# The first layer's squares: POOL adds them in whole tiles, queued behind DVE's splits of the input

## The chip, the cores and the metric

The kernel runs on one core of a Trainium2 chip. The metric is the device time of one execution in microseconds (us); the median of three executions of the kernel before is 2201.84 us (2200.74 to 2202.67). In what follows PE is the engine for matrix products (TensorE), DVE is VectorE, ACT is ScalarE, POOL is GpSimd and SP is SyncE, which here only issues transfers. Each engine takes its instructions strictly in the order in which they stand in its queue, and an instruction that waits holds up all that stands behind it on that engine.

## The reference, cut to what matters

The program is a decoder trunk of two layers over 1024 tokens and 1024 features, float32. Only the start of the first layer matters here:

```python
def rmsnorm(x, g):
    xf = x.astype(jnp.float32)
    var = jnp.mean(xf * xf, axis=-1, keepdims=True)
    return (xf * lax.rsqrt(var + EPS)).astype(x.dtype) * g
...
    for l in range(DEPTH):
        h = rmsnorm(x, norm_mix_g[l])
        uv, z, xbc, dt_raw, c_q, c_kv, k_rope = split_cols(h @ w_in[l])
...
        x = x + mix @ w_out[l]
        x = x + squared_relu_mlp(rmsnorm(x, norm_mlp_g[l]), mlp_w1[l], mlp_w2[l])
    return rmsnorm(x, final_norm_g)
```

The row factor rsqrt(var + EPS) is a scalar for each token, so the kernel multiplies x·g by the weights first and scales the product by it afterwards. The sum of squares is thus needed only when the first product is taken out of PSUM.

## The kernel before

The input lies transposed: eight tiles `x` of 128 features by 1024 tokens (m = 0 to 7), each loaded in two halves of 512 tokens. A float32 product is made of three fast products of split numbers: every operand a becomes a_hi (a rounded copy, written by ACT) and a_lo = a - a_hi (written by DVE). For the input this is `norm_in`: ACT writes `hThi` (line 256), and DVE writes `hTlo` (line 257; the profile gives the helper's line, L103). For the weights it is `split`: ACT's `whi` (L115), DVE's `wlo` (L100).

The first product of the layer is `zps`, eight tiles of 128 tokens by 422 columns, 24 matmuls each (8 feature tiles by 3). The first four token tiles (`z_start`) need the first halves of the input alone, the other four (`z_rest`) the second halves too.

Beside the splits, ACT squares each half of each x tile (`sq_half`), and the squares of the eight feature tiles are summed into one tile: 13 additions of 128x512 on POOL and the last one on DVE (L100, `sq<-sq`). PE then sums over the partitions with a product by ones (`pss`, two columns for each of the eight token tiles), DVE makes the reciprocal root from it in thirteen small steps (`rv`, `ry`, `rt`, `rh`), and only then can ACT take the `zps` tiles out of PSUM (`z_evac`: `zt`, `dk`). Behind the first four of these on ACT stand the splits of the weights of the next product, `xbc`. `row_bcast` (`rb`) spreads the row factor by PE.

The order on each engine is set by a scheduler at build time, which simulates the program; within one engine it may move instructions past each other where data allow it. `tc.issue_after(ins)` tells it that what stands in the block goes, on the engine of `ins` alone, behind `ins`.

Of the kernel before, what the change touches and what calls it, by code (L numbers as in the profile page):

```python
# [9 lines left out]
F32 = mybir.dt.float32  # L10
# [8 lines left out]
P = 128  # L19
# [3 lines left out]
KD = D // P  # L23
# [44 lines left out]
def trunk(ctx, tc, x, w_zdk, w_uv, w_f, w_q, w_kv, w_out, w1, w2, gains, pcol, prow, w_s, cst, out):  # L68
# [5 lines left out]
    small = ctx.enter_context(tc.tile_pool(name="small", bufs=4))  # L74
# [4 lines left out]
    def G(dt=F32, name="g"):  # L79
        return gp.tile([P, 1024], dt, tag="g", name=name)  # L80
# [14 lines left out]
    dve = nc.vector  # L95
    pool = nc.gpsimd
    pe = nc.tensor

    def tt(o, a, b, op, eng=None):
        (eng or dve).tensor_tensor(out=o, in0=a, in1=b, op=op)  # L100
# [10 lines left out]
    def f(ap):  # L111
        return ap.bitcast(F32)
# [121 lines left out]
    def weights(n, ahead=0):  # L234
        a = taken[0]
        prefetch(a + n + ahead)
        taken[0] = a + n
        r = loaded[a:a + n]
        for i in range(a, a + n):
            loaded[i] = None  # L240
        return r
# [11 lines left out]
    def norm_in(xm, m, gi, hT, a=0, b=S):  # L253
        hi, lo = (hsl(h, m, a, b) for h in hT)
        g = gcol[:, gi, m:m + 1]
        act.activation(hi, xm[:, a:b], AF.Copy, scale=g)
        stt(lo, xm[:, a:b], g, f(hi), ALU.mult, ALU.subtract)

    def sq_add(acc, xm, m, a=0, b=S):
        sq = G(F32, "sq")  # L260
        act.activation(sq[:, a:b], xm[:, a:b], AF.Square, scale=1.0 / 32.0)
        if m == 0:
            acc.append(sq)
        else:
            tt(acc[0][:, a:b], acc[0][:, a:b], sq[:, a:b], ALU.add, pool if m < KD - 1 else dve)
# [10 lines left out]
    def hsl(h, k, a, b):  # L276
        return h[:, k * S + a:k * S + b]
# [34 lines left out]
    def begin(l):  # L312
        L = Layer()
        L.l = l
        L.hT = (BIG(F32R, "hThi"), BIG(F32R, "hTlo"))
        L.sq = []
        L.zt = list(range(NT)) if l == 0 else [4, 5, 6, 7, 0, 1, 2, 3]
        L.dk = small.tile([P, NT, 38], F32, tag="dk", name="dk", bufs=1)
        L.rh = small.tile([P, NT], F32, tag="rh1", name="rh1", bufs=1)
        return L  # L320

    def z_start(L, k):
        if k == 0:
            L.zo = [PA("zps") for _ in range(4)]
        for t in range(4):
            z_mm(L, L.zo[t], t, k)
# [587 lines left out]
    def half(n):  # L914
        return slice(n * 512, n * 512 + 512)
# [150 lines left out]
    def sq_half(acc, xm, m, n, eng=None):  # L1066
        if m == 0 and acc:
            act.activation(acc[0][:, half(n)], xm[:, half(n)], AF.Square, scale=1.0 / 32.0)
            return
        sq = G(F32, "sq")  # L1070
        act.activation(sq[:, half(n)], xm[:, half(n)], AF.Square, scale=1.0 / 32.0)  # L1071
        if m == 0:
            acc.append(sq)
        else:
            tt(acc[0][:, half(n)], acc[0][:, half(n)], sq[:, half(n)], ALU.add, eng)
# [151 lines left out]
    L = begin(0)  # L1227
    xs = []

    def x_load(n):  # L1230
        while len(xs) < min(n, 2 * KD):
            h, m = divmod(len(xs), KD)
            xs.append(xs[m] if h else G(F32, "x"))
            nc.sync.dma_start(out=xs[m][:, half(h)], in_=x[m * P:(m + 1) * P, half(h)])
# [4 lines left out]
    for m in range(KD):  # L1239
        x_load(m + 4)  # L1240
        if m % 2 == 0:
            (L.wz[m // 2],) = weights(1, 0)
        norm_in(xs[m], m, 0, L.hT, 0, 512)
        sq_half(L.sq, xs[m], m, 0, pool)
        if m >= 1:
            z_start(L, m - 1)
    consts()
    z_start(L, KD - 1)
    for m in range(KD):
        x_load(KD + m + 4)  # L1250
        norm_in(xs[m], m, 0, L.hT, 512, S)
        sq_half(L.sq, xs[m], m, 1, pool if m < KD - 1 else dve)
    xs.clear()
    for l in range(DEPTH):
        last = l == DEPTH - 1
        xsrc = x if l == 0 else xd
# [45 lines left out]
        L = attention(L, l, xsrc).go()  # L1302
# [75 lines left out]
```

## Time and profile before

| | |
|---|---|
| median of three executions | 2201.84 us |
| the profiled execution | 2201.31 us, of which its span is 2199.5 us |
| PE busy | 2171.2 us, 99% of the span |
| DVE, ACT, POOL busy | 1661.8, 1138.0 and 477.2 us |
| mean granted clock of TensorE | 0.997 |

The span runs from the first to the last instruction. Every time of a row is counted from the span's start. A row of several merged instructions gives the start of the first and the time in which one of them ran. "idle before" in square brackets is the time in which the engine stood still ahead of the row, with what ended it.

### The profile page before, as it was taken

To read this page: it belongs to the slowest core of one execution; us is meant where nothing else is said; L and a number is where in the kernel's file an instruction comes from. 1 tells how busy PE (TensorE), PEld (TensorE's weight loads), DVE (VectorE), ACT (ScalarE), POOL (GpSimd) and SP (SyncE) were. 2 spreads that over 40 slices of the span, in tenths; PEclk is the share of its full clock that TensorE was granted. 3 is DMA by queue.
4 is the path that set the end of the run, shared out by engine and by line. 5 is a ranking of instruction groups with operands and counts; after the bars stand their busy time and mean duration, and the time that the engine had idled before them with its cause. 6 is when DMAs were issued, how large, how long until landed. Compare 5 with 4: busy or idle time off the path is not lost.

```text
span 2199.5 us, 28731 instructions
## 1 busy us (share of the span) xinstructions
PE 2171.2 (99%) x10844; PEld 1846.9 (84%) x10844; DVE 1661.8 (76%) x2484; ACT 1138.0 (52%) x1867; POOL 477.2 (22%) x451
## 2 busy tenths in 40 slices
PE   9999999999999999999999999999999999999997
PEld 8888989888888888888898889998888888888886
DVE  7788588888776876767847867878888767677576
ACT  6364477556445445355533625775464453553543
POOL 4152266221010001001301613761110010011002
PEclk9999999999999999999999999999999999999999
DMA  5211301445565546545412113023565565356532
GB/s 175 75 53 57 87 1 48 98 125 138 121 130 138 128 100 140 147 89 125 156 50 70 54 45 75 1 96 68 135 153 122 106 140 147 88 125 144 136 75 77
DMA packets 64922, 222.16 MB, mean 101 GB/s; under 512 B 7600, under 2 KB 7952, under 8 KB 64784
## 3 DMA queue, kind: packets, MB, share of 16 engines
q0 software_dynamic: 20736, 75.51, 20.2%
q1 hardware_dynamic: 44048, 144.83, 19.9%
q8 instruction: 85, 1.39, 0.3%
q14 instruction: 53, 0.43, 0.1%
HBM read 211.87 MB, written 8.44 MB: 100 GB/s over the span
## 4 chain that ended last, share of the span: by engine, by line
PE 93%; DVE 4%; issue 2%; ACT 1%; DMA 1%; POOL 0%; SPq 0%; POOLq 0%; ACTq 0%; DVEq 0%
PE st L1014 60%; PE cqkv L119 5%; PE xbc L119 5%; PE uvps L119 4%; PE av L119 4%; PE sc L119 3%; PE zps L119 2%; PE pTp L805 2%; PE qps L119 2%; PE yps L119 1%; PE vps L119 1%; PE knps L119 1%; DVE hB L103 1%; DMA x<-in_x 1%; DVE mx L767 1%
## 5 line engine op out<-in xcount | busy, mean ns | idle before, releaser
L1014 PE MATMUL st<-bhi,wlo 128*128 128x512 f32 x2016 | 785.1, 389 | 0.0
L1014 PE MATMUL st<-blo,whi 128*128 128x512 f32 x2016 | 785.0, 389 | 0.0
L1014 PE MATMUL st<-bhi,whi 128*128 128x512 f32 x2016 | 778.1, 390 | 2.4 <-ACT bhi L115 2.4
L1014 PEld LDWEIGHTS st<-bhi,whi 128*128 128x128 f32 x2016 | 378.7, 188 | 81.1 <-ACT bhi L115 2.7
L1014 PEld LDWEIGHTS st<-blo,whi 128*128 128x128 f32 x2016 | 378.9, 188 | 78.7 <-DVE blo L100 0.5
L1014 PEld LDWEIGHTS st<-bhi,wlo 128*128 128x128 f32 x2016 | 378.7, 188 | 78.5
L206 POOL DMA_DIRECT2D ssum<-in_w x96 | 84.1, 876 | 937.5 <-DVE wlo L100 387.5
L100 DVE TENSOR_TENSOR wlo<-raw,whi 128x1024 fp32r<-128x1024 f32 (+4 forms) x189 | 237.2, 1256 | 54.2 <-issue 29.8
L100 DVE TENSOR_TENSOR x<-x,st 128x512 f32<-128x512 f32 x296 | 196.7, 683 | 30.2 <-PE st L1014 29.8
L115 ACT CAST bhi<-tsum 128x1024 fp32r<-128x1024 f32 x96 | 101.0, 1052 | 213.9 <-DVE tsum L100 172.9
L115 ACT CAST whi<-raw 128x1024 fp32r<-128x1024 f32 (+4 forms) x189 | 193.9, 1029 | 16.0 <-DVE blo L100 12.3
L107 POOL TENSOR_SCALAR p<-p,sm 128x1024 f32<-128x1024 f32 (+6 forms) x84 | 158.9, 1901 | 113.0 <-DVE sm L790 81.3
L115 ACT CAST whi<-ssum 128x1024 fp32r<-128x1024 f32 x108 | 113.4, 1050 | 116.3 <-DMA ssum<-in_w 50.2
L100 DVE TENSOR_TENSOR wlo<-ssum,whi 128x1024 fp32r<-128x1024 f32 x108 | 132.1, 1223 | 49.9 <-ACT whi L115 28.9
L100 DVE TENSOR_TENSOR blo<-tsum,bhi 128x1024 fp32r<-128x1024 f32 x96 | 117.4, 1223 | 46.7 <-ACT bhi L115 46.3
L119 PE MATMUL av<-pT,vhi 128*128 128x256 f32 x480 | 113.5, 298 | 0.7 <-DVE pT L100 0.4
L1059 ACT ACTIVATE hid<-hid 128x1024 f32<-128x1024 f32 x64 | 67.8, 1060 | 87.0 <-DVE hid L1052 86.8
L1052 DVE CUSTOM_DVE_ANT_0 hid<-st,hid 128x512 f32<-128x512 f32 x96 | 65.3, 689 | 56.3 <-PE st L1014 55.9
L119 PE MATMUL sc<-B 96*128 96x384 f32 (+11 forms) x432 | 100.9, 351 | 3.2 <-ACT p L780 1.9
L100 POOL TENSOR_TENSOR sq<-sq 128x512 f32<-128x512 f32 x44 | 67.0, 1528 | 159.7 <-ACT sq L1071 157.6
L780 ACT ACTIVATE p<-sc,mx 128x512 f32<-128x512 f32 (+3 forms) x144 | 83.3, 583 | 20.7 <-DVE mx L100 14.2
L100 DVE TENSOR_TENSOR blo<-hB,bhi 128x1024 fp32r<-128x1024 f32 x48 | 58.7, 1223 | 46.5 <-ACT bhi L115 46.5
(248 smaller groups left out, 3649.7 us busy)
## 6 DMA issues: line engine op xcount, KB each, us to landing
raw<-in_w SPq DMA_DIRECT2D x128, 512.0 KB, 3.9
ssum<-in_w POOLq DMA_DIRECT2D x96, 512.0 KB, 5.7
ssum<-in_w SPq DMA_DIRECT2D x32, 512.0 KB, 4.5
raw<-in_w POOLq DMA_DIRECT2D x32, 512.0 KB, 7.9
raw<-in_w_f SPq DMA_DIRECT2D x20, 512.0 KB, 3.8
raw<-in_w_out SPq DMA_DIRECT2D x16, 512.0 KB, 3.6
dec<-adr SPq DMA_DIRECT2D x16, 384.0 KB, 3.4
ssum<-in_w_out POOLq DMA_DIRECT2D x12, 512.0 KB, 5.8
```

The costliest lines, as they stand in the source:

```text
L100: (eng or dve).tensor_tensor(out=o, in0=a, in1=b, op=op)
L103: dve.scalar_tensor_tensor(out=o, in0=a, scalar=s, in1=b, op0=op0, op1=op1)
L107: (eng or dve).tensor_scalar(out=o, in0=a, scalar1=s1, scalar2=None, op0=op0)
L115: act.copy(hi, src)
L119: pe.matmul(o, lhsT=l, rhs=r, start=start, stop=stop)
L206: pool.dma_start(out=o, in_=src, accum_op=ALU.add)
L767: dve.reduce_max(mx[:, n:n + 1], on, axis=AX.X, negate=True)
L780: act.activation(pw[:, n * wh:(n + 1) * wh], os[n][:, :wh], AF.Exp, bias=mx[:, 0:1], accum_out=sm[:, n:n + 1])
L805: pe.transpose(pt[:, c0:c0 + P], pp[j][:, kt * P:(kt + 1) * P], ident)
L1014: pe.matmul(os[j], lhsT=w[:, cw], rhs=b[:, cb], start=first and n == 0, stop=last and n == 2, skip_group_check=True)
L1052: dve._custom_dve(TENSOR_ADD_SAT, out=d, in0=os[j], in1=d, s0=0.0 if full[0] else BIGGEST, s1=-BIGGEST if full[0] else 0.0)
L1059: act.activation(d, d, AF.Square)
```

## The change

The squares no longer follow each half of the input. After all splits have been queued, one POOL instruction copies a single column out of the second half of `hTlo` of feature tile 5 (`mark`), so it has to wait for that split. All POOL additions of squares are queued behind it, and squares and additions are now whole tiles of 128x1024 (`sq_add`, which the kernel already had): eight squares on ACT, six additions on POOL, one on DVE.

```diff
     for m in range(KD):
...
         norm_in(xs[m], m, 0, L.hT, 0, 512)
-        sq_half(L.sq, xs[m], m, 0, pool)
         if m >= 1:
             z_start(L, m - 1)
...
         norm_in(xs[m], m, 0, L.hT, 512, S)
-        sq_half(L.sq, xs[m], m, 1, pool if m < KD - 1 else dve)
-    xs.clear()
+    mark = small.tile([P, 1], F32, tag="mark", name="mark", bufs=1)
+    behind = pool.tensor_copy(mark, f(hsl(L.hT[1], 5, 512, 513)))
+    with tc.issue_after(behind.ins):
+        for m in range(KD):
+            sq_add(L.sq, xs[m], m)
+            xs[m] = None
```

On POOL, at the start of the program, the queue differs as follows (- before, + after; `wst` and `Cz` are later work). The row `L100 ISA` is an instruction that the build puts ahead of POOL's first tensor_tensor: it reloads POOL's library of routines.

```order
+L1377 UNCONDITIONAL_BRANCH
+L1252 COPY mark<-hTlo 128x1
 L100 ISA
-L100 TENSOR_TENSOR sq<-sq 128x512 x13
+L100 TENSOR_TENSOR sq<-sq 128x1024 x6
 L100 TENSOR_TENSOR wst<-wst,cs 128x512
 L416 MEMSET Cz 64x1024 x2
```

Before, the reload was POOL's first work behind the branch and the additions came straight after it; now both stand behind `mark`.

On ACT, from the weights' casts to the second half of feature tile 5, the queue of the changed kernel reads so (`x_105`, `x_110`, `x_112`, `x_114`, `x_132`, `x_152`, `x_174` and `x_190` are the feature tiles 0 to 7; the rows show the stretch from tile 5's first half on, without the two casts of constants that follow `sq_306`).

```order
L256 ACTIVATE hThi_101<-x_152,gcol_75 128x512
L256 ACTIVATE hThi_101<-x_105,gcol_75 128x512
L261 ACTIVATE sq_301<-x_105 128x1024
L256 ACTIVATE hThi_101<-x_110,gcol_75 128x512
L261 ACTIVATE sq_303<-x_110 128x1024
L256 ACTIVATE hThi_101<-x_112,gcol_75 128x512
L261 ACTIVATE sq_306<-x_112 128x1024
```

Behind these stand the two casts of constants, `hThi` of tiles 6 and 7 (first halves), `hThi` and the square of tile 3, `hThi` and the square of tile 4, and then `hThi` of tile 5's second half. Only POOL's instructions are queued behind `mark`; ACT's squares stand among the splits as before, five whole ones ahead of that `hThi`.

On PE, around the matmuls that read the sum of squares, before (the last four of eight `pss`; the name in brackets is the engine whose semaphore is waited for):

```order
L119 MATMUL zps<-whi,hThi 128x422
L119 MATMUL pss<-ones,sq 128x2 [waits DVE_49]
L119 MATMUL pss<-ones,sq 128x2 x3
L119 MATMUL zps<-wlo,hThi 128x422
L119 MATMUL zps<-whi,hTlo 128x422
```

and in the changed kernel (all eight `pss`):

```order
L119 MATMUL zps<-whi,hTlo 128x422
L119 MATMUL pss<-ones,sq 128x2 [waits DVE_49,PE_49]
L119 MATMUL pss<-ones,sq 128x2 x7
L119 MATMUL zps<-whi,hThi 128x422 [waits DVE_49]
L119 MATMUL zps<-wlo,hThi 128x422
```

Before, four `pss` stood further up and four here, with 38 `zps` behind them; now all eight stand in one place, with 24 `zps` (the last token tile) behind them, whose first waits for DVE's reading of `pss`. Later in the program only some neighbours in the attention stages of both layers change places.

## Rows read from the trace of the kernel before

**Rows 1.** The page's head and its row on PE.

```profile
span 2199.5 us, 28731 instructions
PE 2171.2 (99%) x10844; PEld 1846.9 (84%) x10844; DVE 1661.8 (76%) x2484; ACT 1138.0 (52%) x1867; POOL 477.2 (22%) x451
```

**Rows 2.** What PE waited for in the first 60 us: total, times, longest.

```profile
PE zps L119 <- DVE hTlo L103: 0.7, 1, 0.7
PE zps L119 <- DVE wlo L100: 0.5, 1, 0.5
```

**Rows 3.** POOL in order of time: start, us, then the instructions.

```profile
9.21 1.34 POOL L100 TENSOR_TENSOR sq<-sq 128x512 f32<-128x512 f32 x1 [8.77 <-ACT sq L1071]
11.86 7.46 POOL L100 TENSOR_TENSOR sq<-sq 128x512 f32<-128x512 f32 x4 [1.30 <-ACT sq L1071]
20.95 13.83 POOL L100 TENSOR_TENSOR sq<-sq 128x512 f32<-128x512 f32 x8 [1.64 <-ACT sq L1071]
```

**Rows 4.** DVE's splits of the input in order of time.

```profile
4.90 0.75 DVE L103 SCALAR_TENSOR_TENSOR hTlo<-x,gcol,hThi 128x512 fp32r<-128x512 f32 x1 [3.89 <-ACT hThi L256]
...
20.14 11.61 DVE L103 SCALAR_TENSOR_TENSOR hTlo<-x,gcol,hThi 128x512 fp32r<-128x512 f32 x8
```

**Rows 5.** By tile: duration in ns of one, min/median/max (sq; then x).

```profile
L100 POOL TENSOR_TENSOR sq<-sq x44: 1276/1618/2000, 9.2 to 2173.8; 128x512 f32<-128x512 f32 x44
...
L103 DVE SCALAR_TENSOR_TENSOR hTlo<-x,gcol,hThi x16: 737/1770/1786, 4.9 to 33.6; 128x512 fp32r<-128x512 f32 x16
```

**Rows 6.** PE in order of time: the last pss, and xbc's first use of wlo.

```profile
39.33 0.95 PE L119 MATMUL pss<-ones,sq 128*128 128x2 f32 x8
...
50.19 0.62 PE L119 MATMUL xbc<-hThi,wlo 128*128 128x512 f32 x2
```

**Rows 7.** The chain that ended last, its piece behind the last pss.

```profile
40.27 7.37 PE zps L119 x38
```

**Rows 8.** ACT in order of time, first 50 us.

```profile
4.14 0.72 ACT L256 ACTIVATE hThi<-x,gcol 128x512 fp32r<-128x512 f32 x1 [1.82 <-DMA x<-in_x]
...
14.87 0.73 ACT L256 ACTIVATE hThi<-x,gcol 128x512 fp32r<-128x512 f32 x1 [0.61 <-DMA x<-in_x]
...
19.18 0.28 ACT L169 CAST ident_r<-cs 128x128 fp32r<-128x128 f32 x1
...
19.57 0.72 ACT L256 ACTIVATE hThi<-x,gcol 128x512 fp32r<-128x512 f32 x1
20.20 0.61 ACT L1071 ACTIVATE sq<-x 128x512 f32<-128x512 f32 x1
20.71 0.71 ACT L256 ACTIVATE hThi<-x,gcol 128x512 fp32r<-128x512 f32 x1
...
42.99 0.58 ACT L372 ACTIVATE zt<-zps,rh 128x384 f32<-128x384 f32 x1 [14.33 <-DVE rh L107]
...
47.42 2.07 ACT L115 CAST whi<-raw 128x1024 fp32r<-128x1024 f32 x2
49.30 0.68 ACT L372 ACTIVATE zt<-zps,rh 128x384 f32<-128x384 f32 x1
```

**Rows 9.** DVE's split of xbc's first weights.

```profile
48.58 1.23 DVE L100 TENSOR_TENSOR wlo<-raw,whi 128x1024 fp32r<-128x1024 f32 x1 [0.42 <-ACT whi L115]
```

**Rows 10.** By tile, 128x1024: a POOL addition (csq), a DVE subtraction (blo).

```profile
L100 POOL TENSOR_TENSOR csq<-csq x6: 2356/2410/2424, 197.5 to 1324.4; 128x1024 f32<-128x1024 f32 x6
...
L100 DVE TENSOR_TENSOR blo<-tsum,bhi x96: 1215/1225/1228, 505.6 to 2168.1; 128x1024 fp32r<-128x1024 f32 x96
```

**Rows 11.** Behind a wait of PE in layer 1: timeline, window (busy, clock), weight loads.

```profile
1580.72 1.16 PE L119 MATMUL rb<-cs,ry 128*128 128x128 f32 x8 [1.71 <-DVE ry L103]
...
1582.20:1585.60 3.40, 3.40 (x10) 0.50 0.37 148
...
L1014 PEld LDWEIGHTS st<-bhi,wlo x15: 187/188/331, 1574.9 to 1589.7; 128*128 128x128 f32 x15
```

## The prediction

> **What bounds the kernel now.** I read the page first. PE is busy for 2171.2 of 2199.5 us [rows 1], so the time is PE's work plus its few idle stretches, and nothing that happens on POOL, DVE or ACT counts unless PE has to wait for it. All of the change lies in the first 50 us, so I then read what PE waits for there. That is little: 0.7 us for a split of the input (`hTlo`) and 0.5 us for a split of weights [rows 2]. This is the most that the change can win, about 1.2 us, or 0.05%.
>
> The timelines of POOL and DVE show what makes these splits late. Alone, a split takes 0.75 us [rows 4], and its shortest is 737 ns; the median of the sixteen is 1770 ns [rows 5]. Eight in a row take 11.61 us from 20.14 on [rows 4], 1.45 each, while eight POOL additions run beside them for 13.83 us, 1.73 each [rows 3], against a shortest of 1.276 [rows 5]. The two slow each other. So DVE would be served if POOL kept still. But the sum of squares has its own reader: PE's last `pss` begin at 39.33 [rows 6], and behind them the chain goes on through DVE's root and ACT's `zt`, which starts at 42.99 after 14.33 us of standing still [rows 8]. The question is when the additions end now, and what PE has left to do until then.
>
> **The change part by part.**
>
> *Squares on ACT.* Eight whole squares replace sixteen halves. Two halves at a pace of 0.51 (20.20 to 20.71) are 1.02 us; a whole tile, priced by the two casts of 128x1024 that take 47.42 to 49.30, is 0.94 [rows 8]. That wins ACT some 0.6 us in all, on an engine that PE doesn't wait for: nothing on the path.
>
> *When `mark` is free.* It waits for DVE's split of tile 5's second half. ACT's `hThi` of that half sets it, as DVE, without POOL beside it, keeps up. ACT last waits for a transfer at 14.87; between there and this `hThi` stand eight `hThi` at 0.63 (19.57 to 20.20), five whole squares at 0.94 and two casts of constants at 0.39 together (19.18 to 19.57) [rows 8]: 5.04 + 4.70 + 0.39 = 10.1, so it starts at 25.0. A split of the input ends 1.51 after its `hThi` starts (4.14 to 4.90 + 0.75) [rows 4, 8]: 26.5. The copy of one column is of no weight.
>
> *The reload of POOL's library.* This is the part that neither the title nor the diff shows. Before, it lay in the 8.77 us in which POOL idles ahead of its first addition [rows 3], and that addition waited for ACT's square, so the reload cost nothing. Now it stands behind `mark`, and the additions behind it. Its price L has no row: it lies between 0 and 8.8 us, the gap that hid it. No duration in the trace is of the same kind, so I take the middle, 4.4, and keep both ends.
> The Trainium skill has a price (GPSIMD Engine Reference, section Instruction dispatch): the first call after a library is loaded pays about 6 us that no instruction in the profile shows. The trace neither bears this out nor excludes it, since the gap of 8.77 us would have hidden it [rows 3]; by that figure the sum below ends near 2212.5.
>
> *Six additions.* A POOL addition of 128x1024 takes 2.36 to 2.42 us [rows 10]: six make 14.4. They start at 26.5 + L and end at 40.9 + L. If L is under about 3 us, the last two splits run beside them; each such split stretches a half-tile addition from 1.28 to 1.74 [rows 3, 5], so 0.9 more; with L = 4.4 they are past, and DVE has nothing else to do. DVE's own last addition of 128x1024 is 1.22 [rows 10]. The sum of squares is ready at 42.1 + L.
>
> *PE until then.* Before, it came to the last four `pss` at 39.33 [rows 6], with 38 `zps` behind them [rows 7]. Now 24 stand behind them, so 14 more come before: 14 x 0.194 (7.37 / 38) = 2.7 us. Against this, four `pss` are no longer among them (0.95 us for four [rows 6]) and the waits of 1.2 us [rows 2] are gone. PE arrives at about 39.9 and stands still for 2.2 + L us, 6.6 with L = 4.4.
>
> *Behind the wait.* Eight `pss` in place of four: 1.9 us. From the end of `pss` (40.27 [rows 7]) the old chain took until 49.81 to have the first `wlo` of `xbc` (48.58 + 1.23 [rows 9]): DVE's root, four `zt` on ACT, the cast, the split, 9.54 us. Before, PE had 38 `zps` to fill this; now it has 24, 4.7 us, and `rb`, and it waits again, for the weights. PE used that `wlo` at 50.19 [rows 6]; it will do so at 42.1 + L + 1.9 + 9.5 = 53.5 + L. The loss is 3.3 + L.
>
> *The clock.* Elsewhere a wait of PE of 1.71 us was followed by a granted clock of 0.50, the lower of the two levels (1.2 GHz), for 3.4 us, and a weight load took up to 331 ns in place of 187 [rows 11]. After a wait of 6.6 us I expect the same. The eight `pss`, which are mostly weight loads, then take 1.9 x 331 / 187 = 3.3 us, 1.4 more. The `zps` behind them get slower too, but PE is early for `xbc`, which hides that. Bounds: 0, and 2.6 if all the 3.4 us go at a pace of 331 to 187 and ACT's chain doesn't hide it, with a second fall at the wait for the weights.
>
> *The rest of the program.* PE's other waits follow from its own products, so a delay here is carried to the end; the few matmuls that change places in attention I cost at nothing, give or take 1 us: what hides them is that PE has a queue of other matmuls there, and without it they would cost a fraction of a us each.
>
> **The sum.** 3.3 + 4.4 + 1.4 = 9.1 us. The profiled execution took 2201.31, 0.5 under the median; 2201.84 + 9.1 = 2211.0 us, 0.4% slower.
>
> **The rivals.**
>
> *The reload is cheap* (L under 3). For it: nothing in the rows shows such a load, and no transfer is needed if the routines are there already. Then the loss is 3.3 + 0.9 + 1.4 = 5.6 with L = 0, 2207.4; without the fall of the clock 4.2, 2206.0. It is still a loss, since POOL alone needs 14.4 us.
>
> *PE doesn't wait at all* (the other side). The splits come earlier, PE's 1.2 us of waits go, and the additions end in time: 2201.84 - 1.2 = 2200.6, no change that can be measured. It decides at an end of the additions at 39.9 - 1.2 = 38.7, so at (38.7 - 26.5) / 6 = 2.0 us each with no reload at all. Against it stand six rows with 2.36 as the shortest [rows 10].
>
> *It is worse than summed*: the reload fills the whole gap of 8.8, or the clock falls twice, or late `zt` keep PSUM tiles that PE wants. 3.3 + 8.8 + 1.4 = 13.5, 2215.3; with 2.6 for the clock 2216.5.
>
> **How the numbers follow.** The forecast (L from 3 to 8) has 0.57, the cheap reload 0.26, no wait 0.06, the worse one 0.11. Two runs of this kernel can be told apart by about 0.2%, 4.4 us: faster means under 2197.4, slower over 2206.2. No case goes under 2197.4; I leave 0.02 for what the attention stages may do. The cheap reload without a fall of the clock lies just under 2206.2 and takes a fifth of its 0.26; with the case without a wait that makes 0.11 for the same, and 0.87 for slower. The range from 2205.5 to 2215.5 holds the forecast, the cheap reload and a part of the worse one.
>
> **What the changed profile would show.** Right: POOL's six additions of about 2.4 us each, the first one some us after `mark`; the splits on DVE at 0.75 us, the last before 31; one wait of PE of over 4 us at `pss` for DVE's `sq`, a second, shorter one at `xbc` for ACT's `whi` or DVE's `wlo`, and from there on the same intervals as before. L is the gap on POOL between `mark` and the first addition. Wrong: additions that end before 39, a PE that doesn't stand still at `pss`, or a delay at 50 us that is gone again at the end.

## The result, and the profile after

The changed kernel takes 2215.37 us (median of 4 executions, 2212.5 to 2215.74), the kernel before 2201.36 in the same comparison: a ratio of 1.0062, 95% interval 1.005 to 1.0075. The change costs 14.0 us. Behind the forecast of 2211.0 stood a loss of 9.1; the time is inside the range and near its upper end. The profiled execution took 2215.74 us.

The page of the changed kernel, head and row on PE (for [rows 1]):

```profile
span 2214.0 us, 28706 instructions
PE 2180.9 (99%) x10844; PEld 1851.3 (84%) x10844; DVE 1654.6 (75%) x2484; ACT 1138.6 (51%) x1859; POOL 470.5 (21%) x445
```

The span is 14.5 us longer, but PE's busy time grew by 9.7 us with the same 10844 matmuls. A wait alone would leave the busy time as it was, so some of the matmuls must have become slower.

POOL in order of time, 20 to 50 us (for [rows 3]):

```profile
27.11 0.19 POOL L1252 COPY mark<-hTlo 128x1 f32<-128x1 f32 x1 [26.67 <-DVE hTlo L103]
27.34 15.55 POOL L100 TENSOR_TENSOR sq<-sq 128x1024 f32<-128x1024 f32 x6
```

The six additions begin 0.04 us after the copied column ends (27.11 + 0.19 = 27.30), although the reload of POOL's library stands between the two.

DVE in order of time, 26 to 48 us (for [rows 4]):

```profile
26.29 0.75 DVE L103 SCALAR_TENSOR_TENSOR hTlo<-x,gcol,hThi 128x512 fp32r<-128x512 f32 x1 [0.81 <-ACT hThi L256]
27.86 2.43 DVE L103 SCALAR_TENSOR_TENSOR hTlo<-x,gcol,hThi 128x512 fp32r<-128x512 f32 x1 [0.81 <-ACT hThi L256]
30.21 2.46 DVE L107 TENSOR_SCALAR cw<-pc 128x25 f32<-128x25 f32 x2
32.59 0.74 DVE L103 SCALAR_TENSOR_TENSOR hTlo<-x,gcol,hThi 128x512 fp32r<-128x512 f32 x1
...
42.93 1.23 DVE L100 TENSOR_TENSOR sq<-sq 128x1024 f32<-128x1024 f32 x1 [9.61 <-POOL sq L100]
47.88 0.17 DVE L107 TENSOR_SCALAR rv<-pss 128x8 f32<-128x8 f32 x1 [3.73 <-PE pss L119]
```

The splits take 0.75 us each until POOL starts to add; the next one then takes 2.43, and the last one, which starts 0.03 us ahead of POOL's third addition, 0.74 again. That addition by itself:

```profile
32.62 2.95 POOL L100 TENSOR_TENSOR sq<-sq 128x1024 f32<-128x1024 f32 x1
```

DVE then idles 9.61 us until POOL's sixth addition has ended.

What PE waited for in the first 100 us (for [rows 2]):

```profile
PE pss L119 <- DVE sq L100: 5.1, 1, 5.1
PE zps L119 <- ACT whi L115: 0.5, 1, 0.5
PE zps L119 <- DVE rv L107: 0.3, 1, 0.3
```

PE in order of time (for [rows 6]):

```profile
44.30 3.55 PE L119 MATMUL pss<-ones,sq 128*128 128x2 f32 x16 [5.10 <-DVE sq L100]
...
57.44 0.73 PE L119 MATMUL xbc<-hThi,wlo 128*128 128x512 f32 x2
...
64.07 0.63 PE L119 MATMUL xbc<-hTlo,whi 128*128 128x512 f32 x2
...
65.47 0.63 PE L119 MATMUL xbc<-hTlo,whi 128*128 128x512 f32 x2
```

The wait for a split of the input is gone, and a wait of 5.1 us stands at `pss` in its place. The first use of xbc's `wlo` came 7.25 us later than before (50.19 in [rows 6]). That is half of the loss. The other half is not in the first 60 us. The last two rows show where to look: six matmuls start in 1.40 us, 233 ns each. The same product in the trace of before, PE in order of time:

```profile
59.80 0.62 PE L119 MATMUL xbc<-hThi,wlo 128*128 128x512 f32 x2
...
61.63 0.62 PE L119 MATMUL xbc<-hThi,whi 128*128 128x512 f32 x2
```

Eight matmuls in 1.83 us, 229 ns each. The same shows in the table by tile, PE's `xbc` (count, then duration in ns of one, min/median/max), of before and then of the changed kernel:

```profile
L119 PE MATMUL xbc<-hTlo,whi x160: 388/392/397, 49.7 to 1190.2; 128*128 128x512 f32 x160
```

```profile
L119 PE MATMUL xbc<-hTlo,whi x160: 388/395/397, 56.7 to 1202.4; 128*128 128x512 f32 x160
```

And the clock of the changed kernel by windows (length, busy time of PE, PEld, DVE, ACT, POOL, then the granted clock, DMA share, GB/s; for [rows 11]):

```profile
39.30:41.40 2.10, 0.00 (x0) 0.00 (x0) 0.00 (x0) 0.00 (x0) 2.02 (x2) 1.00 0.00 0
41.45:51.60 10.15, 7.04 (x26) 6.81 (x27) 3.41 (x14) 1.03 (x3) 1.44 (x1) 0.50 0.01 2
51.70:55.00 3.30, 3.30 (x21) 3.24 (x21) 2.04 (x9) 3.30 (x11) 0.00 (x0) 1.00 0.00 0
505.55:508.90 3.35, 3.35 (x10) 2.67 (x10) 2.48 (x4) 1.53 (x2) 0.00 (x0) 0.51 0.54 203
1492.15:1495.50 3.35, 3.35 (x10) 2.69 (x9) 3.17 (x5) 2.95 (x6) 1.45 (x1) 0.50 0.44 148
```

The clock fell to its lower level (0.50, 1.2 GHz) while PE stood still at `pss`, and stayed there for 10 us. Two short falls follow later in this execution, where before had one [rows 11]. A short fall costs about 1.6 us (`st` matmuls of 0.43 us from start to start in place of 0.23, eight of them).

What sets the matmuls' pace can't be a wait, since PE is busy throughout. What differs is where the operands lie. In the built kernels the tile pool of the weights (`gp`) lies in SBUF behind the pool of small tiles, and `mark`, 4 bytes per partition, takes 32 there. `hThi` and `hTlo` are 32768 bytes per partition each, a tile of `gp` 4096, all whole multiples of 128, so what is left of a distance when multiples of 128 are taken off (the last column) is the same for every pair of a split input and a weight tile:

```text
byte address per partition    hThi    gp starts   distance mod 128
before                        22336   97536       64
changed                       22336   97568       96
```

So the theory that the experiments were to test has two parts: the order makes PE wait (about half), and the copied column shifts the weights by 32 bytes, which slows the products of the split input (the rest). The rivals: the loss is all due to the wait and what it sets off, or the order is innocent and the whole tiles are what costs.

### The profile page after: what moved, and what is told of

Same layout as the page of the kernel before. It is cut to its first block, busy times and chain, and to the rows that moved or that the text cites. A ratio compares the mean times of both kernels' runs of the same rounds, so it can differ in the third digit from the quotient of the medians.

```text
span 2214.0 us, 28706 instructions
## 1 busy us (share of the span) xinstructions
PE 2180.9 (99%) x10844; PEld 1851.3 (84%) x10844; DVE 1654.6 (75%) x2484; ACT 1138.6 (51%) x1859; POOL 470.5 (21%) x445
## 4 chain that ended last, share of the span: by engine, by line
PE 92%; DVE 3%; issue 2%; ACT 1%; POOL 1%; POOLq 0%; ACTq 0%; DVEq 0%
PE st L1014 60%; PE cqkv L119 5%; PE xbc L119 5%; PE uvps L119 4%; PE av L119 4%; PE sc L119 3%; PE pTp L805 2%; PE qps L119 2%; PE zps L119 2%; PE yps L119 1%; PE vps L119 1%; PE knps L119 1%; POOL sq L100 1%; DVE hB L103 1%; DVE mx L767 1%
## 5 line engine op out<-in xcount | busy, mean ns | idle before, releaser
L100 DVE TENSOR_TENSOR wlo<-raw,whi 128x1024 fp32r<-128x1024 f32 (+4 forms) x189 | 235.2, 1246 | 54.2 <-issue 29.8
L100 DVE TENSOR_TENSOR x<-x,st 128x512 f32<-128x512 f32 x296 | 196.3, 681 | 30.5 <-PE st L1014 30.1
L100 DVE TENSOR_TENSOR wlo<-ssum,whi 128x1024 fp32r<-128x1024 f32 x108 | 131.9, 1221 | 49.7 <-ACT whi L115 27.5
L100 DVE TENSOR_TENSOR blo<-tsum,bhi 128x1024 fp32r<-128x1024 f32 x96 | 117.4, 1223 | 46.6 <-ACT bhi L115 46.3
L780 ACT ACTIVATE p<-sc,mx 128x512 f32<-128x512 f32 (+3 forms) x144 | 83.3, 583 | 21.0 <-DVE mx L100 14.5
L100 DVE TENSOR_TENSOR blo<-hB,bhi 128x1024 fp32r<-128x1024 f32 x48 | 58.7, 1222 | 46.5 <-ACT bhi L115 46.5
L100 POOL TENSOR_TENSOR sq<-sq 128x512 f32<-128x512 f32 (+1 forms) x37 | 60.3, 1634 | 147.6 <-ACT sq L1071 145.8
```

The lines of the kernel that those rows point to most:

```text
L780: act.activation(pw[:, n * wh:(n + 1) * wh], os[n][:, :wh], AF.Exp, bias=mx[:, 0:1], accum_out=sm[:, n:n + 1])
```

## The experiments

**Shifts alone.** First, the changed kernel with 64 bytes in place of 4 for the copied column:

```diff
-    mark = small.tile([P, 1], F32, tag="mark", name="mark", bufs=1)
-    behind = pool.tensor_copy(mark, f(hsl(L.hT[1], 5, 512, 513)))
+    mark = small.tile([P, 16], F32, tag="mark", name="mark", bufs=1)
+    behind = pool.tensor_copy(mark[:, 0:1], f(hsl(L.hT[1], 5, 512, 513)))
```

> The changed kernel, with the copied column in a tile of 64 bytes a partition in place of 4, so that the tiles laid out behind it in SBUF stand 64 bytes further on than in the kernel before, and not 32. Theory A (the shift by 32 bytes is what makes the matmuls of xbc and cqkv start every 233 ns in place of 229): they start every 229 ns again, the creep of about 4 us over these four stages is gone, and the time is near 2211. The start of the program stays: PE waits about 5.1 us at pss, and the first use of xbc's wlo is at about 57.4. Theory B (another cause, such as other buffers or other neighbours in the queues): 233 ns stay, and the time is near 2215. A fall of the clock more or less behind the waits of the later stages moves either by 1.6 us.

Measured: 2206.95 us (1.0025 of before, 1.0015 to 1.0035), 8.4 under the changed kernel. PE in order of time, and its `xbc` by tile:

```profile
43.78 3.55 PE L119 MATMUL pss<-ones,sq 128*128 128x2 f32 x16 [5.05 <-DVE sq L100]
...
57.72 0.62 PE L119 MATMUL xbc<-hThi,wlo 128*128 128x512 f32 x2
```

```profile
L119 PE MATMUL xbc<-hTlo,whi x160: 389/389/398, 57.2 to 1197.3; 128*128 128x512 f32 x160
```

The wait and the late `wlo` are unchanged, and 8.4 us went all the same, by faster matmuls: 389 ns, under the 392 of before. That is twice the 4 us that the expectation had, since it counted on the 229 ns of before and not on a pace that before never had. Then the kernel before, with nothing but a tile of 4 bytes added:

```diff
+    pad = small.tile([P, 1], F32, tag="mark", name="mark", bufs=1)
+    pool.memset(pad, 0.0)
```

> The kernel before, with one more 4-byte tile that POOL sets to zero at the start, so that everything laid out behind it stands 32 bytes further on; no queue is changed otherwise. Theory A (the shift slows xbc and cqkv): matmuls of these two every 233 ns in place of 229, 960 of them, so 4 us more, near 2205.5, and nothing changed before 49 us. Theory B (it was something else): 229 ns, and 2201.4. A fall of the clock more or less moves either by 1.6 us.

Measured: 2206.69 us (1.0022, 1.0013 to 1.0032). PE's `xbc` by tile:

```profile
L119 PE MATMUL xbc<-hTlo,whi x160: 392/396/397, 49.9 to 1194.8; 128*128 128x512 f32 x160
```

An unused tile costs 5.6 us, with no new wait in the first layer. With 64 bytes, `[P, 16]`, in place of 4:

> The kernel before, with 64 unused bytes per partition ahead of the tiles of the weights and no other change; the squares are as before. Theory A (the place of the weights in SBUF sets the pace of the matmuls): as under the changed kernel with 64 bytes, the matmuls of xbc and cqkv go at about 227 ns from start to start in place of 229, some 1.7 us in each layer, 2197.5 us, 0.998. Theory B (the changed kernel's gain with 64 bytes had to do with its own 32 bytes alone, and nothing is below the pace of before): 229 ns and no change, 2201.1.

Measured: 2198.64 us (0.9988, 0.9979 to 0.9997), 2.5 us faster. PE's `xbc` by tile:

```profile
L119 PE MATMUL xbc<-hTlo,whi x160: 389/389/398, 48.3 to 1188.2; 128*128 128x512 f32 x160
```

These four kernels make a table in which the two parts add:

| us | weights shifted by 32 bytes | by 64 bytes | what 32 costs over 64 |
|---|---|---|---|
| squares as before | 2206.69 | 2198.64 | 8.1 |
| squares as changed | 2215.37 | 2206.95 | 8.4 |
| what the new order of squares costs | 8.7 | 8.3 | |

Against the unshifted kernel before, 5.6 us of the 14.0 belong to the shift and 8.3 to 8.7 to the squares. The rival that it is all the wait is refuted.

Two more shifts, one execution each, ask what the pace depends on. 96 bytes ahead of the weights (`[P, 24]`):

> The kernel before with 96 unused bytes ahead of the tiles of the weights. Theory A (32 bytes modulo 64 is what is slow): the matmuls of xbc and cqkv go at 233 ns from start to start and the time is near 2206, as with 32 bytes. Theory B (the nearer to a whole multiple of 128 the input and the weights lie to each other, the faster): with 96 bytes they are 32 apart, as near as with 32 bytes but on the other side, which also gives 233. Either is refuted by a pace of 227 to 229. The run tells whether the pattern is of period 64.

64 bytes ahead of nearly everything, so that weights and split input move together:

```diff
+    pad = const.tile([P, 16], F32, name="pad")
+    pool.memset(pad[:, 0:1], 0.0)
```

> The kernel before with 64 unused bytes ahead of all tiles but the first constants, so that weights and split input move together. If the distance between the two counts: pace as before, 229 ns for xbc and cqkv and 233 for uvps, 2201. If the place of the weights alone counts: as with 64 bytes ahead of the weights alone, 227 and 228.6 ns, 2198.5. A third outcome (slower than 229) would say that the input's place counts too.

Measured: 2205.92 and 2200.8 us. PE's `xbc` by tile, with 96 bytes and then with all moved:

```profile
L119 PE MATMUL xbc<-hTlo,whi x160: 392/395/399, 47.7 to 1192.6; 128*128 128x512 f32 x160
```

```profile
L119 PE MATMUL xbc<-hTlo,whi x160: 388/392/398, 47.9 to 1190.0; 128*128 128x512 f32 x160
```

96 bytes are as slow as 32, and when both operands move by 64, nothing changes, while 64 for the weights alone gave 389. So in these runs the distance between the two operands counts, not the place of either: modulo 128, a distance of 0 gives 389 ns, 64 gives 392, and 32 or 96 give 395 to 396. That is `xbc`'s pattern. `uvps`, another product of the split input, has it only in part: it was slow before already and gains at a distance of 0 alone. Before, and then with 64 bytes ahead of the weights:

```profile
L119 PE MATMUL uvps<-whi,hTlo x128: 388/394/398, 105.6 to 1253.1; 128*128 128x512 f32 x128
```

```profile
L119 PE MATMUL uvps<-whi,hTlo x128: 387/389/402, 103.7 to 1250.2; 128*128 128x512 f32 x128
```

The products `st`, whose operands lie in `gp` both and so at a distance of 0, keep a mean of 389 to 391 ns whether the weights are shifted or not. That fits; distances that differ by 128 bytes alone were not run, so the period of 128 is a reading of these four distances.

**All additions on DVE**, in whole tiles and in the queue's old place, without a copied column (weights not shifted):

```diff
-            tt(acc[0][:, a:b], acc[0][:, a:b], sq[:, a:b], ALU.add, pool if m < KD - 1 else dve)
+            tt(acc[0][:, a:b], acc[0][:, a:b], sq[:, a:b], ALU.add, dve)
```

> The squares as whole tiles as in the changed kernel, but all seven additions on DVE, no copy to wait for and no POOL addition in the first layer; the layout is that of the kernel before. Theory A (what costs is that POOL needs about 15 us from the fifth second-half split on): DVE adds a tile in 1.15 to 1.22 us between its splits, the sum is ready by about 34, PE comes to pss at about 39 to 40 and does not wait, the first use of xbc's wlo comes 0.5 to 1.5 us earlier than the 50.2 of before, and the time is 2200 to 2201.4. Rival (the splits are held up by DVE's additions, so that PE waits for hTlo instead): waits of PE for hTlo of over 1 us before 35, and a time of 2202 to 2204.

Measured: 2201.02 us (0.9998, 0.9989 to 1.0008). DVE's last addition, and what PE waited for in the first 100 us:

```profile
30.90 1.22 DVE L100 TENSOR_TENSOR sq<-sq 128x1024 f32<-128x1024 f32 x1
```

```profile
PE warm L119 <- DVE eps L162: 1.1, 1, 1.1
PE xbc L119 <- ACT whi L115: 0.3, 1, 0.3
```

On DVE an addition of a whole tile takes 1.22 us against 2.4 on POOL [rows 10], and the sum is ready 12 us earlier than in the changed kernel. Both waits of before are gone, and xbc's first `wlo` came at 48.92, 1.3 us earlier than 50.19. The total did not move. The clock doesn't explain that: each of the two traces has one short fall, this one near 392 and before near 1582. But the 1.3 us are no sure gain either: in the four kernels that keep the squares as before and only shift tiles, the same matmul came at 50.39, 48.76, 48.15 and 48.33, so single traces differ there by 2 us.

**The wait filled.** The kernel with 64 bytes, with 24 unused matmuls ahead of `pss` for PE to do while it waits, and token tile 6 as the last one of `zps`:

```diff
     def sq_rstd(acc, tag, t0=0, t1=NT, tg="c", fill=None):
         n = t1 - t0
         pss = bank(tg, "pss")
+        if fill:
+            for _ in range(24):
+                mm(pss[:, 64:486], hsl(fill[1], 7, 512, 640), hsl(fill[0], 7, 512, 934), True, True)
```

> The changed kernel with the 64-byte tile, and 24 matmuls whose results are not used put into PE's wait ahead of pss (the token tiles of the first layer are queued in the order 4, 5, 7, 6, which is the order that the scheduler made anyway). Theory A (the clock fell because PE stood still, and the eight pss at the lower clock cost 3.55 us in place of 1.75): no fall of the clock near 41, pss in about 1.75 us, the first use of xbc's wlo at about 55.6 in place of 57.4, and the time 1.5 to 2 us under that of the same kernel without the filling. Rival (the clock's fall is hidden behind ACT's chain, or pss take 3.5 us for another reason): 57.4 and no difference.

Measured: 2206.39 us (1.0022, 1.0013 to 1.0032). PE in order of time, then a window (columns as above):

```profile
39.34 4.78 PE L119 MATMUL pss<-hThi,hTlo 128*128 128x422 f32 x24
44.05 1.95 PE L119 MATMUL pss<-ones,sq 128*128 128x2 f32 x16
...
55.57 0.73 PE L119 MATMUL xbc<-hThi,wlo 128*128 128x512 f32 x2
```

```profile
46.45:49.80 3.35, 3.35 (x10) 3.17 (x11) 1.83 (x11) 1.08 (x3) 0.00 (x0) 0.50 0.00 0
```

With PE busy until 44.05, the eight `pss` took 1.95 us in place of 3.55, so the lower clock had cost 1.6 there; xbc's `wlo` came 2.15 us earlier (57.72 to 55.57). A shorter fall came none the less, a little later. The median moved only 0.56 us, inside the interval, so of the clock only these 1.6 us on `pss` are shown, and not what it costs the whole.

**The order, or the whole tiles?** Whole tiles on POOL without the order, without the copied column (weights not shifted):

```diff
     for m in range(KD):
         x_load(KD + m + 4)
         norm_in(xs[m], m, 0, L.hT, 512, S)
-    mark = small.tile([P, 1], F32, tag="mark", name="mark", bufs=1)
-    behind = pool.tensor_copy(mark, f(hsl(L.hT[1], 5, 512, 513)))
-    with tc.issue_after(behind.ins):
-        for m in range(KD):
-            sq_add(L.sq, xs[m], m)
-            xs[m] = None
+    for m in range(KD):
+        sq_add(L.sq, xs[m], m)
+        xs[m] = None
```

> Whole squares, six additions on POOL and one on DVE, as in the changed kernel, but not ordered behind the splits, and without the copied column, so that the tiles lie as before. If the order is what makes PE wait: POOL adds while the squares come, the sum is ready before 39, PE doesn't stand still at pss for more than a few tenths, 2201 us, within 0.1 per cent. If the whole tiles do it (POOL's first addition can only begin with the second half of tile 1, and its additions stretch beside DVE's splits to 3 us or more): the sum is ready near 43, PE waits 3 us at pss, 2204.5 to 2206.

Measured: 2210.82 us (1.0037, 1.0025 to 1.005), five executions from 2205.87 to 2211.05; the profile is of the first, at a mean granted clock of 0.997, the longest had 0.993. POOL, DVE, and PE's waits in the first 60 us:

```profile
18.24 16.43 POOL L100 TENSOR_TENSOR sq<-sq 128x1024 f32<-128x1024 f32 x6 [17.80 <-ACT sq L261]
```

```profile
18.81 17.07 DVE L103 SCALAR_TENSOR_TENSOR hTlo<-x,gcol,hThi 128x512 fp32r<-128x512 f32 x7 [0.81 <-ACT hThi L256]
```

```profile
PE zps L119 <- DVE hTlo L103: 3.4, 2, 1.9
PE xbc L119 <- ACT whi L115: 1.4, 1, 1.4
```

Both theories fall short here. The sum is ready in time and PE doesn't wait at `pss`, but the splits beside the whole-tile additions take 2.4 to 2.9 us each, against 0.75 alone (the row has six of them and one behind POOL's last addition, 2.44 on average), and PE waits for the splits, 3.4 us, and for weights. So the order does what it was made for: whole tiles on POOL without it cost about as much, by another wait. The trace is of the fastest execution, 4.7 us over before; what the slower ones have on top of it is not shown. Next, the order with halves in place of whole tiles (64 bytes):

```diff
     with tc.issue_after(behind.ins):
-        for m in range(KD):
-            sq_add(L.sq, xs[m], m)
-            xs[m] = None
+        for n in range(2):
+            for m in range(KD):
+                sq_half(L.sq, xs[m], m, n, pool if m < KD - 1 or n == 0 else dve)
```

> Halves of the squares as before, ordered behind the split of tile 5 as in the changed kernel, with 64 bytes for the copied column. If the order is what makes PE wait: 13 additions of 1.28 us behind the copied column take 16.6 us in place of 14.4, the sum is ready about 1 us later than with whole tiles and 64 bytes, whose wait was 5.05 us, so the wait is 5 to 6.5 us and the time 2207 to 2208.5. If the whole tiles are what costs: the wait is under 3 us and the time under 2204.

Measured: 2206.78 us (1.0027, 1.0016 to 1.0038). POOL and PE in order of time:

```profile
27.77 17.06 POOL L100 TENSOR_TENSOR sq<-sq 128x512 f32<-128x512 f32 x13
```

```profile
44.88 3.57 PE L119 MATMUL pss<-ones,sq 128*128 128x2 f32 x16 [5.55 <-POOL sq L100]
```

The same time as with whole tiles and the same wait: behind the copied column, POOL needs 15.6 to 17.1 us for the sum in either form.

**The reload.** One POOL addition of a single column at the start of the program draws the reload there (64 bytes):

```diff
+    mark = small.tile([P, 16], F32, tag="mark", name="mark", bufs=1)
+    pool.memset(mark[:, 1:2], 0.0)
+    tt(mark[:, 2:3], mark[:, 1:2], mark[:, 1:2], ALU.add, pool)
```

> The changed kernel with 64 bytes for the copied column, and one POOL addition of a single column at the start of the program, so that POOL's library is reloaded there and no longer behind the copied column. Theory A (the reload costs nothing that the program waits for, as the 0.04 us between the copied column and the first addition say): nothing moves, the first wlo of xbc stands near 57.7 and the time is 2207, 1.0025 of before. Theory B (the reload hides in the first addition, which would be longer than the other five): the sum of squares is ready earlier by what it costs, 0.5 us or more, and so is the first wlo of xbc.

Measured: 2206.52 us (1.0024, 1.0014 to 1.0033). POOL in order of time:

```profile
0.91 0.19 POOL L100 TENSOR_TENSOR mark<-mark 128x1 f32<-128x1 f32 x1
26.29 0.19 POOL L1254 COPY mark<-hTlo 128x1 f32<-128x1 f32 x1 [25.18 <-DVE hTlo L103]
26.44 15.57 POOL L100 TENSOR_TENSOR sq<-sq 128x1024 f32<-128x1024 f32 x6
```

Without the reload ahead of them the six additions take 15.57 us, with it 15.55, and the time is that of the kernel with 64 bytes. The reload costs no more than 0.1 us here, neither ahead of the first addition nor inside it. One sign speaks for the other theory: xbc's first `wlo` came at 55.97, 1.75 us earlier than 57.72.

```profile
43.41 2.94 PE L119 MATMUL pss<-ones,sq 128*128 128x2 f32 x16 [4.64 <-DVE sq L100]
...
55.97 0.69 PE L119 MATMUL xbc<-hThi,wlo 128*128 128x512 f32 x2
```

But only 0.37 of this was there when `pss` began (43.41 for 43.78), of which 0.28 are the copy's earlier start (26.29 for 26.57). The rest came behind it: the clock's fall lasted 6.8 us here, 44.1 to 50.9, and 10.2 in the kernel with 64 bytes. At the start of the program too, the first addition follows the memset ahead of it (0.73 + 0.10) within 0.1 us, with the reload between them.

**Two sums.** The order kept (64 bytes), but POOL adds only tiles 0 to 3, DVE tiles 4 to 7, and then the two sums:

```diff
-        if m == 0:
+        if m % 4 == 0:
             acc.append(sq)
         else:
-            tt(acc[0][:, a:b], acc[0][:, a:b], sq[:, a:b], ALU.add, pool if m < KD - 1 else dve)
+            tt(acc[m // 4][:, a:b], acc[m // 4][:, a:b], sq[:, a:b], ALU.add, pool if m < 4 else dve)
...
+        half_b = L.sq.pop()
+        tt(L.sq[0], L.sq[0], half_b, ALU.add, dve)
```

> The changed kernel with 64 bytes for the copied column, in which POOL, behind the copied column, adds only the squares of tiles 0 to 3 (three additions), DVE those of tiles 4 to 7 between and behind its splits (three), and then the two sums (one). Theory A (the loss is six POOL additions in a row behind the copied column): POOL is done at 27.3 + 3 x 2.6 = 35.1, DVE, beside it, at 38 to 40 with the last addition, PE waits at pss 0 to 1.5 us in place of 5.05, and the time is 2199 to 2202.5, where before with 64 bytes had 2198.6. Theory B (what costs is that the whole tiles come late or that all eight pss stand behind them): PE still waits over 3 us and the time is over 2205.

Measured: 2202.06 us (1.0005, 0.9995 to 1.0014). POOL, and PE's waits in the first 100 us:

```profile
26.45 9.68 POOL L100 TENSOR_TENSOR sq<-sq 128x1024 f32<-128x1024 f32 x3
```

```profile
PE xbc L119 <- ACT whi L115: 1.4, 1, 1.4
PE zps L119 <- DVE hTlo L103: 1.3, 1, 1.3
```

The wait at `pss` is gone, and with it 4.9 us against the kernel with 64 bytes. What is left of the loss, 3.4 us over 2198.64, goes with small waits for the last splits and for weights, 2.7 us in this trace. So the row of six POOL additions behind the copied column is the cause of the wait, and the place of the eight `pss` is not.

**Both gains together?** All additions on DVE, and 64 bytes ahead of the weights (the two edits shown above, in one kernel):

> Whole squares, all seven additions on DVE, no order, and 64 unused bytes ahead of the tiles of the weights. Theory A: the two gains add, 1.2 us in the first 50 us (the first wlo of xbc near 48.9) and 3.4 us of pace, 2196.5 us, 0.998; a short fall of the clock more or less moves that by 1.6. Theory B (pace stays at 229 ns): 2201.0, no change, as without the bytes.

Measured: 2199.14 us (0.999, 0.9982 to 0.9999). No second gain shows: the shift alone had xbc's first `wlo` at 48.76 and 2198.64 us, both together had it at 49.13. The 0.5 us between the two totals is no difference that these runs can tell. Both are about 0.1% faster than before, and the simpler of the two is an unused tile of 64 bytes.

## Why the prediction came out as it did

The direction and the place are right, and the total lies in the range; but 9.1 against 14.0 is a sum in which one term didn't occur and another was missing. That the total came this near is in part luck: the 4.4 us that the sum had for a reload that costs nothing happened to stand in for most of the 5.6 of a shift that it did not have.

- **PE has no slack for a later sum: right.** One wait over 4 us at `pss` for DVE's `sq`, as foretold. The second wait, at `xbc`, did not show on PE: slower matmuls on the lower clock filled that time, and only a weight load of `xbc` waited 0.5 us for `wlo`.
- **When `mark` is free, 26.5: roughly right.** The split ended at 27.04 and the copy at 27.30. The forecast had ACT wait for no transfer behind 14.87; its `hThi` of 22.41 did, for 0.62 us. The copy began between 26.22 and 27.53 in the runs with the order, so some of the 0.8 us is scatter.
- **The reload, L = 4.4: this step failed.** The gap that had hidden it (8.77 us, [rows 3]) says nothing about its length; the middle of 0 and 8.8 was a choice without evidence. Measured is 0.04 us, and the run with an early reload shows that the additions hide nothing. With it fell the sign that all splits take 0.75 us and end before 31: the last two ran beside the additions, and the last ended at 33.33. The cheap reload had 0.26 and was the case that occurred. The 6 us that the Trainium skill gives (GPSIMD Engine Reference, section Instruction dispatch) for the first call after a library is loaded did not appear in the two kernels that could show them, the changed one and the one with the early reload.
- **Six additions, 14.4 + 0.9 with splits beside them: right**, 15.55. DVE's addition: 1.22 forecast, 1.23 measured.
- **PE arrives at 39.9, waits 2.2 + L: a little off.** It arrived at 39.20 (44.30 - 5.10). With L = 0 and the 0.9 the wait was to be 3.1 and was 5.10; `mark` gave 0.8 of the 2.0, PE's arrival 0.7, the additions and the steps between them the rest.
- **The clock on `pss`, 1.4: right.** Eight `pss` took 3.55 us, 3.3 were forecast; filling the wait gave 1.6 back.
- **From `pss` to `wlo`, 9.5: right**, 9.6 (47.85 to 57.44).
- **xbc's `wlo` at 53.5 + L.** With L = 0, the 0.9 and the 1.4 that is 55.8; measured 57.44, 1.6 later, by the items above.
- **"From there on the same intervals as before": wrong, and the missing term.** I costed `mark` as a wait and an order, and not as a tile. It moves the weights by 32 bytes, and that alone costs 5.6 us (an unused tile of 4 bytes, measured). By rows: 960 matmuls of `xbc` and `cqkv` (six groups of 160) at 233.3 ns (1.40 / 6) in place of 228.8 (1.83 / 8) are 4.3 us; the rest of the 5.6 is near the price of one short fall of the clock, and that run's profile has one more than before, near 497. Whether most of its executions have it, one profile doesn't show.

The case that happened is the cheap reload, forecast at 5.6 us (2207.4), whose wait measured 8.3 to 8.7 at equal layout, plus 5.6 for a shift that no term of the sum held. Of the 2.7 to 3.1 us by which the wait exceeds 5.6, the items above hold 1.6; the rest stays open. Of the 14.5 us of span, 7.25 stand at `wlo`, 4.3 in the pace and about 1.6 in one more short fall; of the last 1.3, 1.1 lie behind the start of the program's last `rb`, which took 2.07 us in place of 1.31, with the clock at its lower level from its start on, where before it fell in its course. The other traces have 1.6 to 2.1 us there, so this is no doing of the change. How many short falls an execution has varies from run to run, and no run here fixed it.

## What to carry to other kernels

A new tile is never only its bytes: before costing an edit, compare the addresses of the large operands in both builds, since a shift of 32 bytes cost 5.6 us here, where the wait that the change made cost 8.3 to 8.7. A sum that several engines feed should be costed from the moment when its last part may begin, and the order that frees one engine (DVE's splits) needs the queue behind it (six POOL additions of 2.6 us) to be shorter than the work that the waiting engine has left. The length of an idle gap bounds what it may have hidden and is no evidence for any of it, so its middle is no estimate.

## What the runs showed of the hardware that had not been expected

- The pace of `xbc`'s matmuls of 128x512 followed the distance in SBUF between the two operands, modulo 128 bytes: median durations of 389 ns (distance 0), 392 (64) and 395 to 396 (32 and 96), for the same instructions; from start to start, 227 ns (16 matmuls from 60.10 to 63.73 with 64 bytes ahead of the weights), 229 and 233. `uvps` had 389 at a distance of 0 and 394 to 396 at the other three. Shifts of 32, 64 and 96 bytes were run, and one of both operands, all on the split input and the weights; the cause behind it is not shown.
- A DVE instruction that began within a whole-tile addition of POOL ended only behind it, however small: POOL's first addition ended at 29.74 and the split beside it at 30.29 (2.43 us in place of 0.75); the second at 32.55 and the first `cw` of 128x25 at 32.59 (2.37 in place of 0.17). In the run without the order each of the six splits that began so ended 0.55 us behind POOL's addition. The split that began at 32.59, just ahead of the third addition, took 0.74, and that addition 2.95 in place of 2.4. The Trainium skill (SBUF — State Buffer, section SBUF: two separate sides) describes a port pair of DVE and GpSimd that one of them holds for a whole instruction; these rows agree with it.
- After the waits of 5.0 to 5.6 us at `pss` the clock stayed at its lower level for 10 us (41.45 to 51.60 in the changed kernel), after the one of 4.64 for 6.8, and after waits of 1.2 to 1.7 us the fall lasted 3.4. It doesn't follow each of these: every trace has four waits of PE of 1.2 to 1.7 us in the middle of the program, and short falls behind none, one or two of them. With PE kept busy until 44.05 the level was 1.00 through `pss`, and a fall of 3.4 us came at 46.4, after PE's wait of 0.3 us for `rv`.
- The reload of POOL's library, 0.04 us between the instructions on either side of it.
